# Expert weight loads issued from ScalarE in step with the experts, and each gather issued one place earlier on GpSimd

## The chip, the cores and the metric

The kernel runs on one NeuronCore of a Trainium2 chip. The metric is the device time of one execution in microseconds (us); lower is better. Engines are named as the profile names them: PE (TensorE matmul), PEld (TensorE weight load), DVE (VectorE), ACT (ScalarE), POOL (GpSimd), SP (SyncE). A name with a q behind it (ACTq, SPq) is the engine's sequencer, which issues DMAs.

## The reference, cut to what matters

One decoder layer on 1024 tokens of width 1024: a token mixer (stick-breaking attention and gated DeltaNet), then a mixture of experts in which each token goes to 2 of 32 experts. The change lies wholly in the experts:

```python
for gi in range(N_GROUPS):                       # 4 groups of 8 experts
    sl = slice(gi * EXPERTS_PER_GROUP, (gi + 1) * EXPERTS_PER_GROUP)
    h = jax.nn.silu(jnp.einsum("td,edf->tef", x, w1[sl])) * jnp.einsum("td,edf->tef", x, w3[sl])
    y = y + jnp.einsum("tef,efd->td", h * combine[:, gi, :, None], w2[sl])
h = layer_norm(DEEPNORM_ALPHA * h + ffn, ln2_g[i], ln2_b[i])
```

`combine` is zero except for the two experts of a token, so the kernel computes each expert for its own tokens alone.

## The kernel before, in words

Attention, DeltaNet and the routing come first and take the first 815 us or so. Then `phase4` runs a loop over 32 experts, under a manual schedule: instructions stand on each engine in the order in which the code records them. In round `e` of the loop:

- PE multiplies the tokens of expert `e` by its first weights (`up`, into `ph`), then transposes the tokens of expert `e+1` (`xpose`, L1507), then multiplies by the second weights of expert `e-1` (`down`, into `py`).
- ACT and DVE split weights into a high and a low part (`split_k`, L1460 on ACT, L1461 on DVE): `w13h`/`w13l` of expert `e+1`, then `w2h`/`w2l` of expert `e`. Between them they do the gate (`sg`), the split of the tokens (`xh`, `xl`) and the evacuation of expert `e-1` into `y` (L1565 on ACT, L1566 on DVE). There are two buffers of `y` (`YB = 2`).
- POOL issues two indirect DMAs. A gather (L1497) reads the token rows of a later expert from `h1d` into one of three buffers `xg0` to `xg2`, named `XB[0..2]` in the code. A scatter (L1570) adds `y` of expert `e-1` to the rows of those tokens in `res`, in device memory. All scatters write `res`, so each waits until the one before it has landed. A buffer of `y` comes free when the scatter that reads it has landed, so `y` of expert `e` waits for the scatter of expert `e-2`.
- The raw weights of an expert are three chunks of 1 MB: two of `w13`, one of `w2`. There are 96 chunks. `load_raw` loads the next chunks in order of use, into a ring of 17 buffers (`RA + RB + 4 + RC`, named `raw`, `wo4h`, `wo4l`, `wo6h`, `wo6l`):

```python
e, c = order[len(self.raws)]
(eng or self.nc.sync).dma_start(raw, self.a["w13"][e][:, c * 4:c * 4 + 4] if c < 2 else self.a["w2"][e])
```

A load waits for the last reader of the chunk that held its buffer before. At the end of round `e` the program has used `5 + 3e` chunks, and the kernel before asks for all loads up to 17 chunks beyond that. It does so on SP, a queue that has nothing else to do then, so that each load goes out when its buffer comes free. Nineteen chunks are asked for ahead of the loop.

After the loop, SP reads `res` back (L1636), PE adds the last two experts to it (L1737), DVE and ACT do the last layer norm, and SP stores the output.

Of the kernel before, what the change touches and what calls it, by code (L numbers as in the profile page):

```python
# [45 lines left out]
XN = 3  # L46
# [12 lines left out]
RA, RB, RC = 5, 6, 2  # L59
# [20 lines left out]
class Trunk:  # L80
# [1392 lines left out]
    def phase4(self):  # L1473
        nc, a, tc = self.nc, self.a, self.tc
# [21 lines left out]
        def gather(x, xi):  # L1496
            nc.gpsimd.indirect_dma_start(out=x, out_offset=None, in_=self.h1d,  # L1497
                                         in_offset=bass.IndirectOffsetOnAxis(ap=xi, axis=0),
                                         bounds_check=SEQ - 1, oob_is_err=False)

        def xpose(x):
            tps = []
            for g in range(2):
                tp = ps.tile([P, 4, P], F32, name="tp", bufs=2)
                for j in range(4):
                    kt = g * 4 + j
                    nc.tensor.transpose(tp[:, j], x[:, kt * P:(kt + 1) * P], self.ident)  # L1507
                tps.append(tp)
            return tps

        def xsplit(tps):
            xh = mp.tile([P, KT, P], F32R, name="xh", bufs=1)
            xl = mp.tile([P, KT, P], F32R, name="xl", bufs=1)
            xf = mp.tile([P, len(NAT), P], F32, name="xf", bufs=1)
            n = [sum(g * 4 <= k < g * 4 + 4 and k not in NAT for k in range(KT)) for g in range(2)]
            nc.vector.tensor_copy(xf, tps[1][:, n[1]:])  # L1516
            for g in range(2):
                self.split(tps[g][:, :n[g]], xh[:, g * 4:g * 4 + n[g]], xl[:, g * 4:g * 4 + n[g]])
            return xh, xl, xf

        def up(x, pieces):
            xh, xl, xf = x
            ph = ps.tile([P, F], F32, name="ph", bufs=2)
            for i, kt in enumerate(NAT):
                nc.tensor.matmul(ph, xf[:, i], pieces[kt], start=(i == 0), stop=False)
            ks = [kt for kt in range(KT) if kt not in NAT]
            for kt in ks:
                wh, wl = pieces[kt]
                nc.tensor.matmul(ph, xh[:, kt], wh, start=False, stop=False)  # L1529
                nc.tensor.matmul(ph, xh[:, kt], wl, start=False, stop=False)  # L1530
                nc.tensor.matmul(ph, xl[:, kt], wh, start=False, stop=(kt == ks[-1]))  # L1531
            return ph

        def swiglu(ph):
            sg = mp.tile([P, DE], F32, name="sg", bufs=1)
            nc.scalar.activation(sg, ph[:, :DE], AF.Sigmoid)
            nc.vector.tensor_tensor(sg, ph[:, :DE], sg, op=ALU.mult)
            nc.vector.tensor_tensor(sg, ph[:, DE:], sg, op=ALU.mult)
            return sg

        def apose(sg):
            tp = ps.tile([P, 2, P], F32, name="ta", bufs=1)
            for j in range(2):
                nc.tensor.transpose(tp[:, j], sg[:, j * P:(j + 1) * P], self.ident)
            ah = mp.tile([P, 2, P], F32R, name="ah", bufs=1)
            al = mp.tile([P, 2, P], F32R, name="al", bufs=1)
            self.split(tp, ah, al)
            return ah, al

        def down(act, pieces):  # L1550
            ah, al = act
            yo = []
            for s in range(2):
                py = ps.tile([P, F], F32, name="py", bufs=3)
                for j in range(2):
                    wh, wl = pieces.pop(KT + j * 2 + s)
                    nc.tensor.matmul(py, ah[:, j], wh, start=(j == 0), stop=False)
                    nc.tensor.matmul(py, ah[:, j], wl, start=False, stop=False)
                    nc.tensor.matmul(py, al[:, j], wh, start=False, stop=(j == 1))
                yo.append(py)  # L1560
            return yo

        def evac(yo, gv):
            y = mp.tile([P, D], F32, name="y", bufs=YB)
            nc.scalar.activation(y[:, :F], yo[0], AF.Copy, scale=gv)  # L1565
            nc.vector.tensor_scalar(y[:, F:], yo[1], gv, None, op0=ALU.mult)  # L1566
            return y

        def scatter(y, yi):
            nc.gpsimd.indirect_dma_start(out=self.res, out_offset=bass.IndirectOffsetOnAxis(ap=yi, axis=0),  # L1570
                                         in_=y, in_offset=None, bounds_check=SEQ - 1, oob_is_err=False,
                                         compute_op=ALU.add)

        def evac2(yo, gv, y):
            for s in range(2):
                yh, yl = [v[:, s * F:(s + 1) * F] for v in y]
                nc.scalar.activation(yh, yo[s], AF.Copy, scale=gv)
                nc.vector.scalar_tensor_tensor(yl, yo[s], gv, yh.bitcast(F32), op0=ALU.mult, op1=ALU.subtract)
# [3 lines left out]
        def gat_(e):  # L1582
            if e < NE:
                gather(XB[e % XN], self.ix[:, e:e + 1])

        self.load_raw(RX)
        for e in range(XN):
            gat_(e)
        xt = xsplit(xpose(XB[0]))
        self.load_raw(2 + RC - RX)  # L1590
        for e in range(NE):
            more = e + 1 < NE
            gat_(e + XN)
            ph = up(xt, pcs[e])
            if more:
                self.split_k(self.raws_of(e + 1), range(KT), pcs.setdefault(e + 1, {}))
                tps = xpose(XB[(e + 1) % XN])
                sg = swiglu(ph)
                xt = xsplit(tps)
                if e > 0:  # L1600
                    yo, yi = down(act, pcs.pop(e - 1)), self.ix[:, e - 1:e]
                    scatter(evac(yo, self.gsl[:, e - 1:e]), yi)
                act = apose(sg)
                self.split_k(self.raws_of(e), range(KT, 12), pcs[e])
            else:
                self.split_k(self.raws_of(e), range(KT, 12), pcs[e], (), True)
                for i in (1, 0):
                    nc.vector.tensor_tensor(oh[i], self.slots[:, None, :].to_broadcast([P, NT, P]),
                                            ixt[:, i, :, None].to_broadcast([P, NT, P]), op=ALU.is_equal)
                sg = swiglu(ph)  # L1610
                yo = down(act, pcs.pop(e - 1))
                act = apose(sg)
                ys = [[mp.tile([P, D], F32R, name=n, bufs=b) for n, b in (("y", YB), ("xg1", 1))]]
                evac2(yo, self.gsl[:, e - 1:e], ys[0])
            self.load_raw(max(0, 5 + 3 * e + RA + RB + 4 + RC - len(self.raws)))
            if e == NE - 6:
                tb = self.small.tile([P, NT], F32, name="tb", bufs=1)
                nc.gpsimd.iota(tb, pattern=[[P, NT]], base=0, channel_multiplier=0,
                               allow_small_or_imprecise_dtypes=True)
                ixt = self.small.tile([P, 2, NT], F32, name="ixt", bufs=1)  # L1620
                for i in range(2):
                    nc.gpsimd.tensor_copy(ixt[:, i], self.ix[:, NE - 2 + i:NE - 1 + i].to_broadcast([P, NT]))
                    nc.gpsimd.tensor_tensor(ixt[:, i], ixt[:, i], tb, op=ALU.subtract)
            if e == NE - 2:
                oh = [xp.tile([P, NT, P], F32R, name=f"xg{i}") for i in (2, 0)]
# [205 lines left out]
```

## Time and profile before

| what | value |
|---|---|
| median of 3 runs | 1222.26 us (1220.83 to 1227.24) |
| the profiled execution's own time | 1214.15 us |
| its span, first to last instruction | 1212.3 us |
| mean granted TensorE clock | 0.953 |
| PE busy | 1087.4 us, 90% |
| DVE busy | 867.2 us, 72% |
| ACT busy | 624.9 us, 52% |
| POOL busy | 375.2 us, 31% |
| DMAs issued from SP (queue q1) | 239.57 MB, 58.8% of 16 engines' span |
| DMAs issued from POOL (queue q0) | 17.28 MB, 6.1% of 16 engines' span |

Times in the rows below count from the span's start. In a timeline row the first number is the start, the second the duration, and the brackets at the end give the time for which the engine sat idle just before and what ended that idle time. A share of busy time is an average over stages that have different limits, so it is read stage by stage.

### The profile page before, as it was taken

What the parts mean: (1) busy time and instruction counts of PE and PEld (TensorE: products, weight loads), DVE (VectorE), ACT (ScalarE), POOL (GpSimd) and SP (SyncE); (2) the same over time, 40 slices, a digit from 0 to 9 for tenths busy, and PEclk for the clock granted to TensorE, in tenths of its full rate; (3) what the DMA queues carried; (4) which work ended last, traced back from release to release, by engine and by line L of the source; (5) the groups of instructions that cost most, each with busy time, mean ns of one, the idle gap of its engine ahead of it and who ended that gap; (6) DMA issues with size and microseconds to landing.
All of it is one profiled execution on the core that took longest, in us unless ns stands there. A gap on an engine that the chain in (4) does not pass through costs nothing. (4 is left out here: it accounts for less than half of the span.)

```text
span 1212.3 us, 19733 instructions
## 1 busy us (share of the span) xinstructions
PE 1087.4 (90%) x7029; PEld 925.1 (76%) x7029; DVE 867.2 (72%) x1588; ACT 624.9 (52%) x1310; POOL 375.2 (31%) x423
## 2 busy tenths in 40 slices
PE   6999999999899989789999999839999899989981
PEld 4999999999899868678777778736776666666661
DVE  7941357889433258888857687877997787887978
ACT  3443346845233244555546453326776566666754
POOL 3523103502000037666624341141222122122325
PEclk9999999999999978999989999958999999999996
DMA  7411124465896478765657672957999999998353
GB/s 284 174 62 44 54 88 124 149 199 177 249 269 206 156 243 234 220 211 152 187 158 192 209 235 101 405 219 238 343 348 333 310 324 324 325 321 270 80 197 139
DMA packets 111285, 259.20 MB, mean 214 GB/s; under 512 B 32804, under 2 KB 62252, under 8 KB 98386
## 3 DMA queue, kind: packets, MB, share of 16 engines
q1 hardware_dynamic: 101680, 239.57, 58.8%
q0 software_dynamic: 9216, 17.28, 6.1%
q8 instruction: 56, 0.92, 0.3%
q10 hardware_dynamic: 290, 1.07, 0.2%
q14 instruction: 43, 0.35, 0.1%
HBM read 205.44 MB, written 68.72 MB: 226 GB/s over the span
## 5 line engine op out<-in xcount | busy, mean ns | idle before, releaser
L184 PE MATMUL pj<-hTh,wfh 128*128 128x346 f32 (+1 forms) x480 | 156.0, 325 | 0.1
L186 PE MATMUL pj<-hTh,wfl 128*128 128x346 f32 (+1 forms) x480 | 155.6, 324 | 0.0
L185 PE MATMUL pj<-hTl,wfh 128*128 128x346 f32 (+1 forms) x480 | 155.6, 324 | 0.0
L1570 POOL DMA_INDIRECT res<-y,ix x30 | 53.4, 1780 | 233.6 <-DVE y L1566 167.1
L879 DVE TENSOR_TENSOR_SCAN mm<-mm,zero 128x272 f32<-128x272 f32 (+3 forms) x64 | 96.1, 1522 | 28.7 <-ACT mm L866 26.1
L184 PEld LDWEIGHTS pj<-hTh,wfh 128*128 128x128 f32 x480 | 90.8, 189 | 0.5 <-issue 0.3
L186 PEld LDWEIGHTS pj<-hTh,wfl 128*128 128x128 f32 x480 | 90.8, 189 | 0.1
L185 PEld LDWEIGHTS pj<-hTl,wfh 128*128 128x128 f32 x480 | 90.7, 189 | 0.2
L1461 DVE TENSOR_TENSOR w13l<-raw,w13h 128x512 fp32r<-128x512 f32 x144 | 88.9, 686 | 0.0
L1529 PE MATMUL ph<-w13h,xh 128*128 128x512 f32 x192 | 88.8, 463 | 0.0
L177 PE MATMUL pj<-wvh,hTl 128*128 128x256 f32 (+3 forms) x280 | 79.1, 286 | 3.6 <-DVE hTl L95 3.6
L176 PE MATMUL pj<-wvl,hTh 128*128 128x256 f32 (+3 forms) x280 | 79.2, 285 | 2.2 <-DVE wvl L95 2.2
L175 PE MATMUL pj<-wvh,hTh 128*128 128x256 f32 (+3 forms) x280 | 79.6, 288 | 0.3 <-ACT hTh L94 0.3
L1460 ACT ACTIVATE w13h<-raw 128x512 fp32r<-128x512 f32 x144 | 77.8, 624 | 0.0
L1531 PE MATMUL ph<-w13h,xl 128*128 128x512 f32 x192 | 75.3, 392 | 0.0
L1530 PE MATMUL ph<-w13l,xh 128*128 128x512 f32 x192 | 75.2, 391 | 0.0
L866 ACT ACTIVATE mm<-z 128x512 f32<-128x512 f32 (+1 forms) x80 | 44.1, 565 | 49.3 <-PE z L864 35.0
L870 POOL TENSOR_SCALAR_AFFINE_SELECT mm<-mm 128x128 f32<-128x128 f32 x64 | 38.6, 613 | 91.9 <-ACT mm L866 91.4
L864 PE MATMUL z<-qk 128*128 128x416 f32 (+6 forms) x224 | 61.9, 382 | 5.4 <-ACT kuw L776 3.6
L94 ACT ACTIVATE xh<-tp 128x512 fp32r<-128x512 f32 x64 | 31.4, 490 | 59.4 <-DVE xf L1516 52.9
L1461 DVE TENSOR_TENSOR w2l<-raw,w2h 128x512 fp32r<-128x512 f32 x96 | 60.0, 688 | 2.1
L870 POOL TENSOR_SCALAR_AFFINE_SELECT be<-be 128x128 f32<-128x128 f32 x64 | 47.4, 750 | 27.3 <-ACT be L867 23.0
(432 smaller groups left out, 2984.7 us busy)
## 6 DMA issues: line engine op xcount, KB each, us to landing
raw<-in_w SPq DMA_DIRECT2D x72, 1024.0 KB, 19.8
qk<-qkd SPq DMA_DIRECT2D x16, 520.0 KB, 5.3
ht<-hscr SPq DMA_DIRECT2D x16, 512.0 KB, 5.2
qk<-qkd SPq DMA_DIRECT2D x16, 392.0 KB, 6.8
kqvd<-y SPq DMA_DIRECT2D x12, 520.0 KB, 2.9
wfr<-in_w_gdn SPq DMA_DIRECT2D x12, 512.0 KB, 3.5
wo4h<-in_w SPq DMA_DIRECT2D x6, 1024.0 KB, 19.8
wo4l<-in_w SPq DMA_DIRECT2D x6, 1024.0 KB, 13.7
```

What stands on the lines that cost most here:

```text
L175: nc.tensor.matmul(o[:p, :n], xh, wh[:, kt, ws], start=(kt == 0), stop=False)
L176: nc.tensor.matmul(o[:p, :n], xh, wl[:, kt, ws], start=False, stop=False)
L177: nc.tensor.matmul(o[:p, :n], xl, wh[:, kt, ws], start=False, stop=(kt == KT - 1))
L184: nc.tensor.matmul(o[:, :n], wh[:, kt], self.hTh[:, kt, c0:c0 + n], start=(kt == 0), stop=False)
L185: nc.tensor.matmul(o[:, :n], wh[:, kt], self.hTl[:, kt, c0:c0 + n], start=False, stop=False)
L186: nc.tensor.matmul(o[:, :n], wl[:, kt], self.hTh[:, kt, c0:c0 + n], start=False, stop=(kt == KT - 1))
L870: nc.gpsimd.affine_select(out=v[:, e - P:e], in_=v[:, e - P:e], pattern=[[-1, P]], compare_op=ALU.is_gt, fill=fill, base=0, channel_multip ...
L879: nc.vector.tensor_tensor_scan(mm[:, c0:c1][:, ::-1], mm[:, c0:c1][:, ::-1], self.zero1.to_broadcast([P, c1 - c0]), 1.0, op0=ALU.mult, op1 ...
L1460: nc.scalar.activation(wh, raw, AF.Copy)
L1461: (nc.gpsimd if k in pool else nc.vector).tensor_tensor(wl, raw, wh.bitcast(F32), op=ALU.subtract)
L1529: nc.tensor.matmul(ph, xh[:, kt], wh, start=False, stop=False)
L1531: nc.tensor.matmul(ph, xl[:, kt], wh, start=False, stop=(kt == ks[-1]))
```

## The change

```diff
         xt = xsplit(xpose(XB[0]))
+        gat_(XN)
         self.load_raw(2 + RC - RX)
         for e in range(NE):
             more = e + 1 < NE
-            gat_(e + XN)
             ph = up(xt, pcs[e])
             if more:
                 self.split_k(self.raws_of(e + 1), range(KT), pcs.setdefault(e + 1, {}))
                 tps = xpose(XB[(e + 1) % XN])
+                gat_(e + 1 + XN)
                 sg = swiglu(ph)
                 xt = xsplit(tps)
...
-            self.load_raw(max(0, 5 + 3 * e + RA + RB + 4 + RC - len(self.raws)))
+            n = RA + RB + 4 + RC - 2
+            self.load_raw(max(0, 5 + 3 * e + n - e * (n - 8) // 28 - len(self.raws)), nc.scalar)
```

The loads of the loop are issued by ACT instead of SP, at the end of each round. `n` is 15, so that after round `e` the program has asked for `20 + 3e - e // 4` chunks: one in round 0, then three in a round, and two in every fourth. The distance to the chunks in use sinks from 15 to 8, and the 96th chunk is asked for in round 28. The gather of expert `e+4` is recorded in round `e`, behind the transposes that free its buffer; before, the gather of expert `e+3` was recorded there.

On ACT, rounds 0 to 2 stand like this before (the last four `w2h` of a round are followed by the six `w13h` of the next):

```order
L1460 ACTIVATE w2h<-raw 128x512 x4
L1460 ACTIVATE w13h<-raw 128x512 x6
L1536 ACTIVATE sg<-ph 128x256
L94 ACTIVATE xh<-tp 128x512
L94 ACTIVATE xh<-tp 128x256
L1565 ACTIVATE y<-py,gsl 128x512
L94 ACTIVATE ah<-ta 128x256
L1460 ACTIVATE w2h<-raw 128x512 x4
L1460 ACTIVATE w13h<-raw 128x512 x6
```

and like this in the changed kernel, from the same row on:

```order
L1460 ACTIVATE w2h<-raw 128x512 x4
L1448 DMA wo6h<-in_w 128x2048
L1460 ACTIVATE w13h<-raw 128x512 x6
L1536 ACTIVATE sg<-ph 128x256
L94 ACTIVATE xh<-tp 128x512
L94 ACTIVATE xh<-tp 128x256
L1565 ACTIVATE y<-py,gsl 128x512
L94 ACTIVATE ah<-ta 128x256
L1460 ACTIVATE w2h<-raw 128x512 x4
L1448 DMA wo6l<-in_w 128x2048
L1448 DMA raw<-in_w 128x2048 x2
L1460 ACTIVATE w13h<-raw 128x512 x6
```

The loads (L1448) now stand between the `w2h` of a round and the `w13h` of the next; 77 of them move from SP to ACT.

On POOL, from the gathers ahead of the loop to the third scatter, before (`xg0` to `xg2` are the three token buffers; the number behind a name is the program's own):

```order
L1497 DMA xg0_8867<-h1d_4815,ix_92 128x1024
L1497 DMA xg1_8869<-h1d_4815,ix_92 128x1024
L1570 DMA res_4816<-y_9091,ix_92 1024x1024
L1497 DMA xg2_8871<-h1d_4815,ix_92 128x1024
L1570 DMA res_4816<-y_9210,ix_92 1024x1024
L1497 DMA xg0_8867<-h1d_4815,ix_92 128x1024
L1570 DMA res_4816<-y_9329,ix_92 1024x1024
```

and in the changed kernel:

```order
L1497 DMA xg0_8867<-h1d_4815,ix_92 128x1024
L1497 DMA xg1_8869<-h1d_4815,ix_92 128x1024
L1497 DMA xg2_8871<-h1d_4815,ix_92 128x1024
L1570 DMA res_4816<-y_9090,ix_92 1024x1024
L1497 DMA xg0_8867<-h1d_4815,ix_92 128x1024
L1570 DMA res_4816<-y_9209,ix_92 1024x1024
L1497 DMA xg1_8869<-h1d_4815,ix_92 128x1024
```

Each gather has moved ahead of one scatter; they still alternate. PE and DVE have the same instructions in the same order as before.

## Rows read from the trace of the kernel before

**Rows 1.** Windows: us; busy and (count) of PE, PEld, DVE, ACT, POOL; PEclk, DMA share, GB/s.

```profile
843.00:907.00 64.00, 64.00 (x291) 48.75 (x290) 61.50 (x113) 51.14 (x102) 18.32 (x12) 1.00 0.98 345
907.00:1104.00 197.00, 177.10 (x772) 127.11 (x770) 161.28 (x296) 125.38 (x258) 46.12 (x34) 1.00 0.95 323
1127.00:1160.00 33.00, 32.02 (x145) 24.21 (x144) 31.58 (x58) 26.55 (x54) 14.98 (x11) 1.00 0.34 61
```

**Rows 2.** Timeline of PE: the transposes of two experts, early in the loop.

```profile
877.52 1.03 PE L1507 MATMUL tp<-ident,xg 128*128 128x128 f32 x8
887.18 1.03 PE L1507 MATMUL tp<-ident,xg 128*128 128x128 f32 x8
```

**Rows 3.** Timeline of POOL: scatters (L1570) and one gather (L1497), first to last.

```profile
844.25 1.86 POOL L1570 DMA_INDIRECT res<-y,ix  x1 [10.91 <-ACT w2h L1460]
...
924.26 1.59 POOL L1570 DMA_INDIRECT res<-y,ix  x1 [8.59 <-DVE y L1566]
926.16 1.04 POOL L1497 DMA_INDIRECT xg<-h1d,ix  x1 [0.31 <-issue]
935.85 1.60 POOL L1570 DMA_INDIRECT res<-y,ix  x1 [8.65 <-DVE y L1566]
...
1117.44 1.59 POOL L1570 DMA_INDIRECT res<-y,ix  x1 [8.47 <-DVE y L1566]
...
1128.38 1.59 POOL L1570 DMA_INDIRECT res<-y,ix  x1 [8.01 <-DVE y L1566]
...
1135.48 1.59 POOL L1570 DMA_INDIRECT res<-y,ix  x1 [1.70 <-DVE w13l L1461]
...
1142.20 3.56 POOL L1570 DMA_INDIRECT res<-y,ix  x1 [3.78 <-DVE w13l L1461]
1151.02 3.92 POOL L1570 DMA_INDIRECT res<-y,ix  x1 [5.26 <-ACT w13h L1460]
1160.14 2.02 POOL L1570 DMA_INDIRECT res<-y,ix  x1 [5.20 <-ACT w13h L1460]
```

**Rows 4.** The scatter line L1570: who waited for it (us, times); its time to landing.

```profile
  ACT y L1565: 33.7, 16
DMA to landing us min/median/max: 5.8/10.4/11.1
```

**Rows 5.** Timeline of ACT in one round of the slow stage.

```profile
934.92 0.69 ACT L1565 ACTIVATE y<-py,gsl 128x512 f32<-128x512 f32 x1 [2.28 <-DMA res<-y,ix]
935.77 2.20 ACT L1460 ACTIVATE w2h<-wo4h 128x512 fp32r<-128x512 f32 x4
946.66 0.69 ACT L1565 ACTIVATE y<-py,gsl 128x512 f32<-128x512 f32 x1 [2.57 <-DMA res<-y,ix]
```

**Rows 6.** Timeline of SP: loads at the loop's start and end, and the read-back.

```profile
836.64 8.31 SPq L1448 DMA_DIRECT2D raw<-in_w  x3
...
1100.16 4.70 SPq L1448 DMA_DIRECT2D raw<-in_w  x2
...
1166.62 4.45 SPq L1636 DMA_DIRECT2D yt<-res  x8
```

**Rows 7.** Timeline of ACT: a DMA that ACT issues at 421 us, and its next activation.

```profile
421.78 0.33 ACTq L649 DMA_DIRECT2D qkd<-qlo  x1
422.06 0.38 ACT L713 ACTIVATE Z<-tp 32x256 f32<-32x256 f32 x1
```

**Rows 8.** Timelines: ACT in a round of the fast stage; DVE behind the loop.

```profile
870.50 0.39 ACT L94 ACTIVATE xh<-tp 128x256 fp32r<-128x256 f32 x1 [1.40 <-DVE xf L1516]
...
1174.22 1.22 DVE L1746 SCALAR_TENSOR_TENSOR yt<-pf,yt 128x1024 f32<-128x1024 f32 x1 [3.67 <-PE pf L1737]
```

**Rows 9.** The gather line L1497: who waited for it (us, times).

```profile
  PE tp L1507: 10.8, 12
```

**Rows 10.** Time to landing of the read-back L1636.

```profile
DMA to landing us min/median/max: 6.0/9.8/11.8
```

**Rows 11.** Time to landing of the weight loads L1448.

```profile
DMA to landing us min/median/max: 4.9/19.7/22.2
```

## The prediction

> **What bounds the kernel now.** The change touches only the loop over the experts, so I read that stage and not the page's shares. First the windows [rows 1]. From 843 to 907 us PE is busy for all of 64.00 us. From 907 to 1104 it is busy for 177.10 of 197.00 us at the same granted clock, and DVE and ACT are further from full than PE. The DMA engines are at 0.98 and 0.95 in the two windows, and at 0.34 once the loads are over. So there is a fast stage, a slow stage, and a quiet end. In the fast stage PE sets the pace, one expert in 887.18 - 877.52 = 9.66 us [rows 2].
>
> What holds back the slow stage is in the timeline of POOL [rows 3]. Scatters start 11.6 us apart (924.26, 935.85), and over the 24 intervals from 844.25 to 1117.44 the mean is 273.19 / 24 = 11.38 us. The first 24 scatters thus keep this pace from the start, while PE still runs at 9.66. Each scatter waits for the one before it to land: the landing takes 10.4 us in the median [rows 4]. A scatter chain slower than PE falls behind by 1.7 us an expert until both buffers of `y` are in use; then ACT stands still in front of `y`, for 2.28 us in one round and 2.57 in the next [rows 5], 33.7 us over 16 rounds [rows 4], and an expert takes as long as a scatter. The bound is the chain of scatters, not PE and not the loads as such.
>
> What makes a scatter slow is seen at the end. After the last loads left SP at about 1105 us [rows 6], the intervals fall to 7.10 and 6.72 us; the next two are 8.82 and 9.12, but there POOL itself spends 3.56 and 3.92 us on the instruction instead of 1.59, and without that surplus they are 6.85 and 6.79 [rows 3]. So a quiet scatter needs about 6.9 us and one beside three loads 11.38: an estimated surcharge of 4.5 us, or 1.5 per load. DMA share matters little beyond that: the interval is 11.4 at 0.98 as at 0.95 [rows 1, 3].
>
> **The change, part by part.** The sum is made against the profiled execution's 1214.15 us. The median of the runs is 8.1 us above that, and I add this at the end.
>
> *Loads in the middle of the loop.* Before, SP sends a load when its buffer comes free, three in a round. Now they leave together behind `w2h`. In the slow stage `y` and the next scatter are let go by the same landing (934.92 and 935.85), and `w2h` ends at 935.77 + 2.20 = 937.97 [rows 3, 5]. So the loads leave 2.1 us behind the scatter's start, and the scatter has landed when the next `y` starts, at 946.66 [rows 5]. At 345 GB/s [rows 1] three loads of 1.05 MB take 9.1 us, until 947: the whole landing still lies beside loads. In such a round I change nothing. In 7 rounds there are only two loads, which take 6.1 us and leave the last 2.6 us of the landing free. That is worth between 0 and the surcharge of one load, 1.5 us; with about half, 7 rounds return 5 us (0 to 10.5).
>
> On this step there is a rule: the Trainium skill, "DMA: Bandwidth & Descriptors", "Queues, rings and completion order", says that each DMA engine takes turns, packet by packet, between the rings that have work. By that rule a scatter cares whether any load is queued beside it, not whether one or five are; and the same page's "Issuing engines are not separate DMA queues" says that issuing from another engine saves only the issuing time. By it alone the middle returns 0 instead of 5 us. That the interval is as long at the start of the loop as later agrees with it [rows 3].
>
> *Loads at the start.* SP sent three loads from 836.64 to 844.95 us [rows 6], beside the first scatter. Now round 0 sends one, and rounds 1 and 2 three each. One or two loads fewer lie beside the first scatters: 2 us back (0 to 4.5).
>
> *Loads at the end.* Chunk 96 is now asked for in round 28, instead of at about 1105 us. The scatters behind 1128.38 and 1135.48, which came 7.10 and 6.72 us apart [rows 3], now get three loads each. At 11.38 they cost 4.3 + 4.7 = 9.0 us (4.3 if one alone is hit).
>
> *What stands behind the last scatter.* The read-back of `res`, which needs the last scatter landed, starts at 1166.62 [rows 6], and the shortest landing is 6.0 us [rows 10], so 1172.6. DVE uses it at 1174.22, and what it waited for is PE, 3.67 us [rows 8]. So the first 1.6 us of lateness cost nothing.
>
> *Issuing from ACT.* No row shows ACT issuing three loads in a row. One DMA on ACT's sequencer takes 0.33 us and runs beside an activation: started at 421.78, it did not keep the next from starting at 422.06 [rows 7]. So three cost between 0 and 1.0 us. In the slow stage ACT idles over 2 us in front of `y` [rows 5], in the fast one 1.40 us in front of `xh` [rows 8]: cover enough, and I take 0. Without cover it would be 1.0 us in some 8 fast rounds, 8 us. A load on ACT also waits for its buffer's last readers; with the distance at 15 or less these are done rounds before.
>
> *The gather.* It is issued one scatter earlier. In the slow stage POOL reaches it right behind a scatter, as before (926.16 behind 924.26 [rows 3]), when the transposes it now waits for are long done; so the next scatter isn't held. PE waited for gathers 10.8 us in 12 waits [rows 9]. That is the most it could return, but PE then waits for the scatter chain instead: 0.
>
> Sum: -5 - 2 + 9.0 - 1.6 = +0.4 us, 1214.6 for the profiled execution and 1222.7 on the scale of the median. A difference under 0.5%, 6.1 us, can't be told from none here.
>
> **The rivals.**
>
> *A, faster: the loads in step get out of the scatters' way.* Rounds with 2.75 loads on average leave the DMA engines idle between bursts: 323 GB/s in 11.38 us is 3.68 MB, less a quarter of a load 3.41 MB, which at 345 GB/s takes 9.9 us [rows 1, 3]. If the scatters fall into the gaps, an expert takes between 9.9 and 11.38 us; halfway, at 10.6, 20 slow rounds return 16 us, and the two late scatters cost 7.4. With the start and the slack: -16 - 2 + 7.4 - 1.6 = -12, 1210; at 9.9 it would be -28, 1194. For it: the gap exists on paper. Against it: the phase, since the same landing that starts a scatter also starts ACT's way to the next burst. The Trainium skill, same page, "Latency and other measured facts", speaks for A: it says that device memory answers faster under lighter load. No row here shows that, since both stages with loads keep 11.4 us.
>
> *B, slower: the late loads alone.* The middle and the start return nothing, and the lateness at the end isn't hidden: +9.0, 1231. It decides if a round with two loads costs a scatter as much as one with three. For it: the turns above. Against it: 1.5 us per load as estimated.
>
> *C, slower: ACT's queue.* If a burst isn't through when the next leaves, the loads' landing grows. It was 19.7 us in the median and 22.2 at most [rows 11], with more loads ahead than now. A burst that had to wait on ACT would hold the split of every weight. Each us beyond the 2 us of cover costs 1 us a round: 20 us at one us in 20 rounds, 1243.
>
> **How the numbers follow.** No change 0.45, A 0.31, B 0.20, C 0.04. The likeliest one's own range is 1217 to 1228: 10.5 + 4.5 returned at most, nothing at least, against 4.3 to 9.0, cut at 0.5% of the median. For 8 in 10 the range must take in A halfway and B whole: 1204 to 1232. Faster by over 0.5% is 0.31, slower 0.24, neither 0.45.
>
> **What would show it.** Right: scatters still some 11.4 us apart through the middle, a little less in every fourth round; ACT still idle 2 us in front of `y`; the quiet intervals at the end gone; load issues of 0.33 us on ACT with no wait behind `w2h`; no wait of PE for gathers. Wrong: intervals near 10 us and no idle time in front of `y` (A), or ACT idle in front of the loads or of `w13h` (C).

## The result, and the profile after

The changed kernel takes 1231.84 us (median of 12 runs) where the kernel before, beside it on the same chip, takes 1220.61 (12 runs): a ratio of 1.008, 95% interval 1.0053 to 1.0107, so slower by 0.8%. The forecast was 1222.7 and "no change" as the likeliest. The time that came lies 0.2 us inside the upper end of the stated range (1204 to 1232), so it is in part luck that the range held; it is also near the 1231 worked out for rival B, but other terms made it up, as the experiments show.

The profiled execution has a span of 1226.2 us, 13.9 more than before. That is more than the 11.2 us between the medians, because the execution profiled before took 1214.15 us, 6.5 below that kernel's median, and the one after lies 2.9 below its own. First the windows of the changed kernel (columns as in [rows 1]): the fast stage, the slow stage, and the end in three pieces.

```profile
845.00:909.00 64.00, 64.00 (x289) 48.50 (x288) 58.10 (x107) 47.35 (x95) 17.59 (x11) 1.00 0.90 320
909.00:1106.00 197.00, 173.95 (x760) 127.33 (x759) 159.19 (x291) 125.38 (x258) 47.04 (x35) 0.98 0.83 297
1106.00:1129.00 23.00, 18.64 (x73) 12.87 (x72) 18.06 (x34) 14.05 (x30) 4.77 (x4) 0.93 0.81 276
1129.00:1152.00 23.00, 21.49 (x97) 16.05 (x96) 18.38 (x35) 14.34 (x31) 7.25 (x9) 1.00 0.94 326
1152.00:1180.00 28.00, 24.63 (x110) 18.19 (x109) 26.28 (x47) 18.61 (x39) 9.46 (x5) 1.00 0.35 66
```

In the slow stage the DMA engines now have gaps, 0.83 of their time instead of 0.95 [rows 1], and PE is busy for 173.95 us of 197 instead of 177.10. The gaps exist, and the pace did not gain by them. The loads are still there from 1129 to 1152, where before the quiet end had begun. The clock granted to TensorE is a little lower as well, 0.98 and then 0.93 where it was 1.00 in the slow stage before [rows 1], and 0.947 over the whole span instead of 0.953; but the run with only the gather moved, below, also has 0.947 and is no slower.

Timeline of POOL in the changed kernel: the first scatter, three of the slow stage, and the end.

```profile
846.77 1.86 POOL L1570 DMA_INDIRECT res<-y,ix  x1 [3.07 <-ACT w2h L1460]
...
1032.51 1.59 POOL L1570 DMA_INDIRECT res<-y,ix  x1 [8.67 <-DVE y L1566]
...
1044.30 1.60 POOL L1570 DMA_INDIRECT res<-y,ix  x1 [8.85 <-DVE y L1566]
...
1055.66 1.59 POOL L1570 DMA_INDIRECT res<-y,ix  x1 [8.42 <-DVE y L1566]
...
1126.56 1.59 POOL L1570 DMA_INDIRECT res<-y,ix  x1 [8.54 <-DVE y L1566]
...
1138.14 1.59 POOL L1570 DMA_INDIRECT res<-y,ix  x1 [8.64 <-DVE y L1566]
...
1149.83 1.59 POOL L1570 DMA_INDIRECT res<-y,ix  x1 [5.82 <-DVE y L1566]
1159.56 1.57 POOL L1570 DMA_INDIRECT res<-y,ix  x1 [8.14 <-ACT y L1565]
1166.13 1.79 POOL L1570 DMA_INDIRECT res<-y,ix  x1 [5.00 <-DVE w13l L1461]
1173.17 4.88 POOL L1570 DMA_INDIRECT res<-y,ix  x1 [5.25 <-DVE w13l L1461]
```

The 24 intervals from the first scatter to 1126.56 take 279.79 us, 11.66 each (before 11.38), and the five behind them 46.61 (before 1160.14 - 1117.44 = 42.70 [rows 3]). Then the read-back, on SP, and DVE's first use of it:

```profile
1182.69 5.28 SPq L1638 DMA_DIRECT2D yt<-res  x8
...
1188.72 1.23 DVE L1748 SCALAR_TENSOR_TENSOR yt<-pf,yt 128x1024 f32<-128x1024 f32 x1 [5.74 <-SPq L1663]
```

The read-back starts 9.52 us behind the last scatter (before 6.48 [rows 3, 6]; POOL spends 4.88 us on that scatter instead of 2.02). DVE now waits for SP, no longer for PE [rows 8]: L1663 is a branch that SP reaches when all eight read-backs are issued, at 1182.69 + 5.28 = 1187.97. So the 13.9 us of these two executions are: 2.5 before the first scatter, 6.6 in the 24 intervals, 3.9 in the last five, 3.0 behind the last scatter, less 2.2 that the rest (43.5 us instead of 45.7) gives back, which is 13.8. The first two need care: in the run with only the gather moved, below, which is no slower, the first scatter is late by 4.4 us and the mean interval is 11.58. One profile does not carry 0.2 us of an interval; the ratios do.

The waits at the scatter line L1570 of the changed kernel, with its landing, and those at the gather line L1497 (who waited: us, times):

```profile
  ACT y L1565: 50.6, 22
DMA to landing us min/median/max: 5.7/10.7/12.6
```

```profile
  PE tp L1507: 7.0, 1
```

ACT stands in front of `y` for 50.6 us instead of 33.7, and the landing takes 10.7 us instead of 10.4 [rows 4]: still the same bound. PE's waits for gathers are gone but for the first (before 10.8 in 12 [rows 9]).

Timeline of ACT in one round of the changed kernel; ACTq is ACT's sequencer, which issues the DMAs:

```profile
1043.51 0.69 ACT L1565 ACTIVATE y<-py,gsl 128x512 f32<-128x512 f32 x1 [2.61 <-DMA res<-y,ix]
1043.74 0.33 ACTq L1448 DMA_DIRECT2D wo6h<-in_w  x1
1044.10 0.38 ACT L94 ACTIVATE ah<-ta 128x256 fp32r<-128x256 f32 x1
1044.11 0.45 ACTq L1448 DMA_DIRECT2D wo6l<-in_w  x1
1044.36 0.63 ACT L1460 ACTIVATE w2h<-raw 128x512 fp32r<-128x512 f32 x1
1044.60 0.44 ACTq L1448 DMA_DIRECT2D raw<-in_w  x1
1044.88 1.67 ACT L1460 ACTIVATE w2h<-raw 128x512 fp32r<-128x512 f32 x3
```

The loads stand behind `w2h` in ACT's order, and yet leave while `y` runs, ahead of `ah` and `w2h`: the first at 1043.74, 0.56 us before the scatter at 1044.30. In the slow stage the first load of a round always leaves 0.2 to 0.7 us before the scatter. I had them 2.1 us behind it.

The round from 1044.30 has three loads, the one from 1055.66 only two. Windows of both, the first 6.5 us behind the scatter and the 3.5 us after these:

```profile
1044.30:1050.80 6.50, 5.96 (x31) 4.68 (x29) 6.20 (x11) 6.13 (x13) 2.64 (x2) 1.00 0.95 360
1050.80:1054.30 3.50, 2.22 (x7) 1.23 (x8) 2.36 (x6) 0.38 (x1) 0.00 (x0) 1.00 0.91 326
1055.66:1062.16 6.50, 6.36 (x33) 5.01 (x31) 6.33 (x11) 6.00 (x13) 3.10 (x2) 1.00 0.96 350
1062.16:1065.66 3.50, 2.35 (x8) 1.32 (x9) 2.23 (x6) 0.38 (x1) 0.00 (x0) 1.00 0.57 170
```

With two loads the DMA engines are at 0.57 in the second stretch instead of 0.91, so the end of the landing is indeed partly free, as the prediction had it. Yet the next scatter starts 11.71 us later (1067.37), against 11.36 in the round with three. All five two-load rounds of the slow stage show this: 0.43 to 0.57 in the second stretch, and no shorter interval on average (the table by rounds, below).

### The profile page after: what moved, and what is told of

Its sections match the earlier page's. It is cut to its first block, busy times and chain, and to the rows that moved or that the text cites. A ratio compares the mean times of both kernels' runs of the same rounds, so it can differ in the third digit from the quotient of the medians.

```text
span 1226.2 us, 19632 instructions
## 1 busy us (share of the span) xinstructions
PE 1091.9 (89%) x7029; PEld 930.1 (76%) x7029; DVE 868.9 (71%) x1588; ACT 624.4 (51%) x1310; POOL 375.8 (31%) x423
## 3 DMA queue, kind: packets, MB, share of 16 engines
q10 hardware_dynamic: 11378, 81.81, 17.5%
## 5 line engine op out<-in xcount | busy, mean ns | idle before, releaser
L1570 POOL DMA_INDIRECT res<-y,ix x30 | 53.2, 1773 | 236.6 <-DVE y L1566 185.4
```

## The experiments

All ratios are against the kernel before, run beside it. "Interval" is the mean of the first 24 between scatters, "last five" the time from the 25th scatter to the 30th, both from one profile.

| run | median us | ratio, 95% interval | interval | last five | ACT's waits for a scatter's landing in front of `y` |
|---|---|---|---|---|---|
| before | 1220.61 to 1225.72, five sets | 1 | 11.38 | 42.70 | 33.7 us, 16 |
| changed | 1231.84 | 1.008, 1.0053 to 1.0107 | 11.66 | 46.61 | 50.6, 22 |
| gather only | 1221.53 | 0.9991, 0.996 to 1.0021 | 11.58 | 38.63 | 29.9, 13 |
| loads only | 1231.60 | 1.0094, 1.0064 to 1.0124 | 11.87 | 46.82 | 45.2, 19 |
| distance 15 | 1227.81 | 1.004, 1.0015 to 1.0065 | 11.65 | 42.33 | 40.3, 18 |
| ahead of `y` | 1223.96 | 1.0011, 0.9982 to 1.004 | 11.35 | 46.02 | 31.0, 15 |
| spread | 1224.04 | 1.0011, 0.9976 to 1.0047 | 11.36 | 45.16 | 41.6, 20 |
| ahead, distance 15 | 1228.74 | 1.0021, 1.0 to 1.0042 | 11.68 | 43.42 | 49.1, 21 |
| no scatters | 1187.34 | 0.970, 0.9663 to 0.9736 | | | none |
| before, halves | 1205.78 | 0.985, 0.981 to 0.9889 | 10.26 | 51.34 | 10.7, 11 |
| before, quarters | 1204.22 | 0.9843, 0.9804 to 0.9883 | 10.22 | 55.05 | none |
| changed, halves | 1233.33 | 1.0063, 1.0043 to 1.0084 | 11.19 | 53.71 | none |
| ahead, 15, halves | 1245.79 | 1.0168, 1.0132 to 1.0203 | 12.06 | 48.05 | none |
| changed, 4 KB rows | 1215.18 | 0.9919, 0.989 to 0.9947 | 10.78 | 49.44 | none |

**Which part of the change.** My theory after the result: the phase, that is, loads that leave in step with the scatters slow the chain. Rivals: the gather; the late end alone; ACT's own issue time. First each half alone.

The gather's move in the kernel before:

```diff
         xt = xsplit(xpose(XB[0]))
+        gat_(XN)
...
-            gat_(e + XN)
...
                 tps = xpose(XB[(e + 1) % XN])
+                gat_(e + 1 + XN)
```

> The kernel before with the gather's move alone; loads on SP as before. Theory 1 (the loads that leave in step with the scatters make the scatter chain slower) expects no change: ratio 0.997 to 1.003, scatters 11.4 us apart in the mean over the first 24 intervals. Rival 2 (the gather that is issued ahead takes the scatter's place) expects the whole loss here: ratio 1.006 to 1.010, 11.6 to 11.7 us apart.

Measured 0.9991, though the interval of its one profile, 11.58, lies nearer to what rival 2 expects. The other half, the loads alone:

```diff
-            self.load_raw(max(0, 5 + 3 * e + RA + RB + 4 + RC - len(self.raws)))
+            n = RA + RB + 4 + RC - 2
+            self.load_raw(max(0, 5 + 3 * e + n - e * (n - 8) // 28 - len(self.raws)), nc.scalar)
```

> The kernel before with the loads on ACT and the sinking distance; gathers as before. Theory 1 expects the whole loss: ratio 1.006 to 1.010, scatters 11.6 to 11.7 us apart over the first 24 intervals, the last five intervals some 4 us longer in sum than in the kernel before. Rival 2 expects ratio 1.000.

Measured 1.0094: the loads carry all of the loss, the gather none.

**How much of it is the sinking distance.** The changed kernel with 15 chunks to the end:

```diff
-            self.load_raw(max(0, 5 + 3 * e + n - e * (n - 8) // 28 - len(self.raws)), nc.scalar)
+            self.load_raw(max(0, 5 + 3 * e + n - len(self.raws)), nc.scalar)
```

> The changed kernel with the distance held at 15 chunks: three loads in every round, the last in round 26. Theory 1 expects the middle as in the changed kernel (11.6 to 11.7 us apart) and an earlier quiet end: 4 us better than the changed kernel, ratio to the kernel before 1.003 to 1.006. Rival 3 (only the late loads at the end cost) expects 11.4 us apart and ratio 1.000.

Measured 1.004, half of the loss, as theory 1 expects; the late loads alone (rival 3) are not enough. The last five intervals fall from 46.61 to 42.33 us, and the read-back starts 6.33 us behind the last scatter instead of 9.52. What the sinking gave elsewhere, rounds with two loads, returned nothing: 11.65 us per interval without them, 11.66 with them.

**The place of the issue.** The same two lines, but ahead of the evacuation into `y`:

```diff
                 xt = xsplit(tps)
+                n = RA + RB + 4 + RC - 2
+                self.load_raw(max(0, 5 + 3 * e + n - e * (n - 8) // 28 - len(self.raws)), nc.scalar)
                 if e > 0:
...
-            n = RA + RB + 4 + RC - 2
-            self.load_raw(max(0, 5 + 3 * e + n - e * (n - 8) // 28 - len(self.raws)), nc.scalar)
```

> The changed kernel with the loads issued by ACT ahead of the evacuation into y instead of at the round's end: ACT stands idle there for 2.5 us, so the loads leave that much ahead of the landing that lets go the next scatter. Theory 1 (the phase is what costs) expects the scatters to lie less beside loads: 10 to 11 us apart, ratio 0.975 to 0.995. The rule of turns (a scatter cares only whether some load is queued, and loads fill the round anyway) expects 11.4 to 11.7 us apart and a ratio of 1.005 to 1.010. Rival 4 (ACT's own time for the issues is the cost) expects the same 1.005 to 1.010, with ACT waiting for y less by as much as its issues take.

Measured 1.0011, 0.7% better than the changed kernel, but short of the 0.975 to 0.995 that my theory expected; the interval is 11.35 us and not 10 to 11. Timeline of ACT in that run, the load issues and `y` alone, over two rounds:

```profile
1036.91 0.33 ACTq L1448 DMA_DIRECT2D wo6h<-in_w  x1
1037.29 0.45 ACTq L1448 DMA_DIRECT2D wo6l<-in_w  x1
1037.77 0.44 ACTq L1448 DMA_DIRECT2D raw<-in_w  x1
1039.89 0.69 ACT L1565 ACTIVATE y<-py,gsl 128x512 f32<-128x512 f32 x1 [2.60 <-DMA res<-y,ix]
...
1048.69 0.82 ACTq L1448 DMA_DIRECT2D raw<-in_w  x2
1052.14 0.69 ACT L1565 ACTIVATE y<-py,gsl 128x512 f32<-128x512 f32 x1 [3.07 <-DMA res<-y,ix]
```

The loads now leave 3 to 3.5 us ahead of `y`. Then the loads of a round one at a time, at three places:

```diff
+        def load(e, left):
+            n = 5 + 3 * e + 15 - e // 4 - left - len(self.raws)
+            self.load_raw(max(0, n), nc.scalar)
...
                 gat_(e + 1 + XN)
+                load(e, 2)
                 sg = swiglu(ph)
                 xt = xsplit(tps)
+                load(e, 1)
...
-            n = RA + RB + 4 + RC - 2
-            self.load_raw(max(0, 5 + 3 * e + n - e * (n - 8) // 28 - len(self.raws)), nc.scalar)
+            load(e, 0)
```

> The changed kernel with the up to three loads of a round no longer issued together: ACT sends one behind the split of w13, one ahead of the y evacuations and one at the end of the round; the distance is the same. Theory 1 (the phase: a burst of three loads that leaves in step with the scatter slows it): the interval falls from 11.66 to about 11.4 us and the ratio to about 1.002. If only the number of loads beside a scatter matters: intervals 11.66 and a ratio of 1.008 as in the changed kernel. If ACT's issuing itself costs: the same or worse, 1.008 to 1.012.

Measured 1.0011 as well. And both losses undone at once, ahead of `y` and 15 chunks to the end (the edit is against the run ahead of `y`):

```diff
-                self.load_raw(max(0, 5 + 3 * e + n - e * (n - 8) // 28 - len(self.raws)), nc.scalar)
+                self.load_raw(max(0, 5 + 3 * e + n - len(self.raws)), nc.scalar)
```

> The changed kernel with both of its two losses undone: the loads are issued 2.5 us earlier, ahead of y (alone 1.0011), and the distance stays 15 chunks (alone 1.004). If the two are separate terms (0.7% for the place, 0.4% for the late end), they add: ratio 0.995 to 0.999, interval 11.35 us, s24 to s29 42 us. If they are one effect seen twice, the ratio stays at 1.001 to 1.004.

Measured 1.0021. If the terms added, it would be 1.0011 + 1.004 - 1.008 = 0.997; the intervals of the four ratios together leave some 0.5%, so this is just at the edge of noise. It speaks against terms that add, and against a phase that costs every round the same. I sorted the intervals between scatters by the loads that ACT issued in them (from 5.5 us before a scatter to 5.5 before the next; one profile each, number of rounds in brackets):

| run | rounds with two loads | rounds with three |
|---|---|---|
| changed | 11.49 us (5) | 11.61 (20) |
| loads only | 11.73 (5) | 11.79 (20) |
| distance 15 | | 11.56 (23) |
| ahead of `y` | 10.65 (6) | 11.59 (19) |
| spread | 10.61 (7) | 11.54 (16) |
| ahead, distance 15 | | 11.68 (23) |

Three loads cost the same within 0.25 us wherever they leave. What the place seems to decide is whether a round with only two is shorter: on average by about 0.9 us when the loads leave earlier or one by one, by 0.1 when they leave with the scatter. These are few rounds and they scatter widely (ahead of `y` the six lie between 9.36 and 12.53 us). If it is so, a constant distance, which has no such rounds, has nothing to win from the better place. Why two loads that leave with the scatter cost as much as three isn't settled by these runs; that the loads fill its whole landing is ruled out by the windows above.

**Is it the scatter chain at all?** The changed kernel without the loop's scatters (the sums of experts 0 to 29 into `res` are left out):

```diff
-                    scatter(evac(yo, self.gsl[:, e - 1:e]), yi)
+                    evac(yo, self.gsl[:, e - 1:e])
```

> The changed kernel without the scatters of the loop: the sums of experts 0 to 29 into res are left out, and nothing else. If the chain of scatters is what holds the loop (the reading of the profile before), PE sets the pace: 9.66 us per expert instead of 11.6, the loop shorter by some 35 to 40 us, ratio 0.965 to 0.975 against the kernel before. If the loads issued by ACT hold it (theory 4: ACT's queue, or the loads' late landing), the intervals stay near 11.5 and the ratio at 1.000 to 1.008.

Measured 0.970. Windows and PE's timeline of that run:

```profile
909.00:1100.00 191.00, 191.00 (x876) 146.67 (x875) 183.06 (x338) 148.76 (x296) 21.87 (x25) 1.00 0.87 329
...
1057.41 1.03 PE L1507 MATMUL tp<-ident,xg 128*128 128x128 f32 x8
1067.07 1.03 PE L1507 MATMUL tp<-ident,xg 128*128 128x128 f32 x8
```

From 909 to 1100 us PE is never idle and takes 9.66 us an expert, with the same loads issued by ACT at the same places. So neither ACT's issuing nor the supply of weights holds the changed kernel; the scatters do.

**What makes a scatter slow.** If a DMA engine serves the loads and the scatter in turns, a scatter's price depends on the size of the load's packet in each turn. So I tried the kernel before, with each load of the loop on SP as two DMAs of half a chunk, or as four of a quarter (1 in the place of the 2):

```diff
-            (eng or self.nc.sync).dma_start(raw, self.a["w13"][e][:, c * 4:c * 4 + 4] if c < 2 else self.a["w2"][e])
+            src = self.a["w13"][e][:, c * 4:c * 4 + 4] if c < 2 else self.a["w2"][e]
+            w = 2 if i > 18 else 4
+            for k in range(0, 4, w):
+                (eng or self.nc.sync).dma_start(raw[:, k:k + w], src[:, k:k + w])
```

> The kernel before, but each load of the loop (a chunk of 1.05 MB, 128 rows of 8 KB) is issued on SP as two DMAs of half a chunk, with rows of 4 KB. The bytes and the place of the loads are the same. Theory by turns (a scatter's packets stand in turn with the loads' packets, and what a turn costs is the size of the load's packet): the scatter's surcharge of 4.5 us beside loads shrinks to about half, intervals of 9.2 to 10.5 us instead of 11.38, ratio 0.975 to 0.990. Theory by bytes (the scatter suffers from the number of bytes queued beside it): intervals 11.4, ratio 1.000. A third way: SP's doubled issuing or the larger number of descriptors costs time, ratio 1.005 or more.

> As the run with halves, with four DMAs of a quarter of a chunk (rows of 2 KB). By turns: surcharge a quarter to a half of 4.5 us, so an interval of 8.0 to 9.2 us, below PE's 9.66: PE would set the pace, the waits of ACT in front of y (33.7 us) would go, and the ratio would be 0.965 to 0.985. By bytes: intervals 11.4, ratio 1.000. With small rows the transfer itself could become slower: then the DMA share stays near 1.0 while GB/s fall below 320, and the ratio is above 1.01.

Measured 0.985 and 0.9843. First the windows of the run with halves, then the landing of its scatters:

```profile
909.00:1100.00 191.00, 186.50 (x836) 140.06 (x835) 176.22 (x323) 140.92 (x285) 51.44 (x38) 0.99 0.93 308
1100.00:1130.00 30.00, 25.79 (x115) 19.08 (x114) 22.27 (x40) 18.34 (x36) 8.35 (x11) 0.99 1.00 325
```

```profile
DMA to landing us min/median/max: 9.1/9.7/9.8
```

The landing falls from 10.4 to 9.7 us and the interval by 1.1, so the direction is that of the turns; the surcharge of 4.5 us was to halve and fell by a quarter. With quarters the first 19 intervals average 9.71, PE's pace, and ACT has no wait for a landing in front of `y`. Both lose part of it at the end (51.34 and 55.05 us for the last five): with halves the DMA engines are at 1.00 there and ACT waits for weights in front of `w13h`. But with smaller DMAs SP also waits for its earlier loads; in the kernel before it waited only for a buffer's readers. The longest of its queue's waits from 845 to 1130 us in the run with halves:

```profile
SPq L1451 <- DMA raw<-in_w: 148.2, 90, 3.5
```

So fewer bytes could be the cause, instead of smaller packets. The same edit on the changed kernel, where ACT issues:

> The changed kernel, but each load that ACT issues in the loop goes out as two DMAs of half a chunk (rows of 4 KB). If the size of the packets beside the scatter sets its price in the changed kernel too, as the run with halves on SP showed for the kernel before (interval 11.38 to 10.26 us, ratio 0.985), the interval falls from 11.66 to about 10.5 us, and the ratio from 1.008 to about 0.990: the whole gain less the late loads at the end (0.4%) and the phase. If the phase alone (a burst that leaves with the scatter) makes the changed kernel slow, the interval stays above 11.3 us and the ratio above 1.002. If ACT's six issues per round (about 2.6 us) are not covered, ACT's idle time in front of y is used up and w13h and w2h come late: ratio above 1.008.

Measured 1.0063, and on the version ahead of `y` with 15 chunks:

> The kernel of the run ahead_const with each loop load as two DMAs of half a chunk, issued by ACT: the place, the distance and the packet size together. By the terms so far (-0.4% and -1.5%) ratio 0.975 to 0.985, interval about 10.2 us, near PE's 9.66. Whether it beats the halves on SP (0.985) depends on ACT's issuing: six issues of about 0.4 us per round ahead of y, where ACT now waits 31 us in 15 rounds for the scatter; with a faster scatter that cover is gone, and uncovered it costs up to 2.6 us in a round, ratio 0.99 to 1.02.

Measured 1.0168. ACT's longest wait behind a DMA in the first of the two from 845 to 1150 us, and then one place in its timeline:

```profile
ACT w13h L1463 <- DMA raw<-in_w: 40.2, 13, 4.4
```

```profile
947.63 1.68 ACT L1463 ACTIVATE w2h<-wo4h 128x512 fp32r<-128x512 f32 x3
950.18 3.49 ACTq L1451 DMA_DIRECT2D raw<-in_w  x3
953.72 2.19 ACT L1463 ACTIVATE w13h<-wo4l 128x512 fp32r<-128x512 f32 x4 [4.40 <-DMA raw<-in_w]
```

The scatters did become faster: their landing is 9.9 us in both runs, and the waits for them in front of `y` are gone. But now ACT stands still while its queue issues: the three loads end at 950.18 + 3.49 = 953.67, and the split of the weights starts at 953.72. The trace names the landing of an earlier load as the cause. In the second run, where the loads stand ahead of `y`, ACT waits there instead, 46.6 us in 16 waits for loads. This is rival C, brought about by twice as many DMAs. On SP the same waits hold nobody up. The last run takes the number of DMAs out of it: one DMA per chunk again, but the two halves of each row change places in the buffer, so that a row goes as two packets of 4 KB:

```diff
+        self.perm = {}
...
-            (eng or self.nc.sync).dma_start(raw, self.a["w13"][e][:, c * 4:c * 4 + 4] if c < 2 else self.a["w2"][e])
+            src, dst = self.a["w13"][e][:, c * 4:c * 4 + 4] if c < 2 else self.a["w2"][e], raw
+            if i > 18:
+                src = src.rearrange("p (h k) d -> p h (k d)", h=2)
+                dst = raw.rearrange("p (h k) d -> p h (k d)", h=2)[:, ::-1]
+            (eng or self.nc.sync).dma_start(dst, src)
+            if i > 18:
+                self.perm[id(raw)] = (2, 3, 0, 1)
...
-            raw = raws[k // 4][:, k % 4]
+            raw = raws[k // 4]
+            raw = raw[:, self.perm.get(id(raw), (0, 1, 2, 3))[k % 4]]
```

> The changed kernel; each load of the loop stays one DMA of a whole chunk, issued by ACT where the change issues it, but the two halves of each row change places in the buffer (and the split reads them there), so that a row of 8 KB goes as two packets of 4 KB. The number of DMAs, and so ACT's issuing and its waits for earlier loads (43 us in front of w13h with two DMAs per chunk), stay as in the changed kernel. If the size of the packets beside the scatter sets the scatter's price, and the run with halves on ACT lost the gain only to ACT's waits, the interval falls from 11.66 to 10.3 to 10.8 us, ACT's 50.6 us in front of y go down to some 10 to 20, and the ratio falls from 1.008 to 0.990 to 0.997. If the gain of the halves on SP came from something else that goes with twice as many DMAs (fewer bytes in flight on SP), or if the phase makes the changed kernel slow, the interval stays at 11.5 or more and the ratio at 1.004 to 1.010.

Measured 0.9919, faster than the kernel before although nothing else of the change is undone. ACT's DMA queue on the page of the changed kernel, and of this one (packets, MB, share of 16 engines):

```profile
q10 hardware_dynamic: 11378, 81.81, 17.5%
```

```profile
q10 hardware_dynamic: 21234, 81.81, 17.9%
```

The same bytes in nearly twice the packets. Of this run also the landing of the scatters, that of the loads (the median ends the row; below it the same row of the run with the loads only, since the trace of the changed kernel has no landing of its loads), and ACT's wait in front of `w13h` from 845 to 1150 us:

```profile
DMA to landing us min/median/max: 6.2/9.7/11.9
```

```profile
raw<-in_w ACTq DMA_DIRECT2D x59, 1024.0 KB, 21.1
```

```profile
raw<-in_w ACTq DMA_DIRECT2D x59, 1024.0 KB, 9.5
```

```profile
ACT w13h L1468 <- issue: 35.0, 12, 4.6
```

The landing is 9.7 us instead of 10.7, the interval 10.78 instead of 11.66, and ACT doesn't wait for a scatter in front of `y`. The loads take 21.1 us to land, 9.5 with rows of 8 KB, so there are not fewer bytes queued beside the scatter: that rival falls, and the size of the packets is the cause of what was gained. It is a part only: with packets of half the size the landing falls by 0.7 us on SP and 1.0 on ACT, while a scatter's shortest landing before was 5.8 [rows 4]. What this version loses, 35.0 us in front of `w13h`, has no releaser in the trace; load issues of up to 5.5 us lie there.

## Why the prediction was right and where it was wrong

**The bound** was right. The run without scatters is PE-bound at 9.66 us, as [rows 2] says, and saves 3.0%.

**The gather, 0 us:** right; alone it gives 0.9991, and PE's 12 waits for gathers went away without a gain.

**Issuing from ACT, 0 us:** right: a median of 0.44 us a load and at most 2.0, beside other work, with no wait of ACT in front of `w13h`, and 9.66 us an expert with the same issues once the scatters are left out. That the loads leave at the end of `w2h` was wrong.

**Loads in the middle, -5 us:** this is the step that failed. It priced a free end of the landing at about half of 1.5 us, and the 1.5 was the surcharge of three loads divided by three: no row showed a round with one or two. The free end came, and longer than said, since the loads leave with the scatter and not 2.1 us behind it; but a round with two loads is 0.1 us shorter than one with three, not 0.7. (There are six such rounds, not seven: round 28 asks for one load.) Issued earlier, such a round was 0.9 us shorter on average, at a place where this change doesn't put the loads. Rival B's condition, that two loads cost a scatter as much as three, held in the changed kernel.

**Start, -2 us:** nothing came. The first three intervals took 36.77 us, before 33.90, but also 36.93 with the loads as before and the gather moved.

**Loads at the end, +9.0, and the slack, -1.6:** the direction was right, the size too large: the distance held at 15 gives back 0.4%, 5 us. In the profile the two intervals that I had named grew by 4.6 and 3.0 us (11.69 and 9.73 instead of 7.10 and 6.72), near the 9.0. But the two behind them shrank by 2.3 and 2.1, since POOL's slow instructions of 3.56 and 3.92 us are not there; one of 4.88 now stands at the last scatter and makes up nearly all of the 3.0 us behind it. The slack was used up as said: the read-back starts 16.1 us later than before and DVE's first use of it comes 14.5 later.

**Rival B** met the time but not the terms: it put all of the loss on the late loads. They account for about half, and a mere earlier issue, with the loads just as late at the end (46.02 us for the last five), takes away nearly all of it.

**What stays.** With the sinking undone the changed kernel is still at 1.004 (1.0015 to 1.0065), and with the better place too at 1.0021 (1.0 to 1.0042). This rest of 0.2 to 0.4% has no shown cause; the three-load intervals of about 11.6 us lie within what single profiles differ by.

**Rival A** fell as it stood: the gaps came (0.83), and the scatter didn't use them. The Trainium skill, "DMA: Bandwidth & Descriptors", "Latency and other measured facts", has memory answer faster under lighter load; at a lighter load on average the landing here was 10.7 us instead of 10.4. The rule of turns in the same page of the Trainium skill ("Queues, rings and completion order") fared better: it has a DMA engine switch between rings only after a whole packet, and the runs with shorter rows agree in kind, at 9.7 to 9.9 us of landing. Whether the unit is the same isn't shown: the page counts several descriptors to a packet, while the trace counts one packet more for each row that is cut in two ((21234 - 11378) / 77 = 128 a load). As the prediction read the rule, two loads would not be cheaper than three, and with an earlier place they were, 10.65 us against 11.59.

## What to carry to other kernels

When a small transfer on the path shares the DMA engines with bulk loads, ask what the loads' packets are before moving the loads about: 4 KB instead of 8 KB was worth 1.5% here, while every move of the loads' place or distance, packets as before, lay between 0 and a loss of 0.9% against the kernel before. DMAs that may have to wait belong on an engine with nothing behind them: the same halves gained 1.5% from SP, and from ACT next to nothing (1.0063, and 1.008 without them). And read the place of an issue from the sequencer's rows, not from the order of the code: it runs ahead of the engine.

## What was not expected of the hardware

ACT's sequencer issued loads that stand behind `ah` and four `w2h` in its order while `y`, ahead of these, was still running: a load started at 1043.74, the first `w2h` at 1044.36. Issuing a load with two packets per row took a median of 0.63 us on ACT instead of 0.44. The last scatter cost POOL 4.88 us in the changed kernel against 1.59 for most: the two others well above it that [rows 3] shows also lie at the loop's end, and what they share isn't known.
